# Window attention scores as stacked high and low halves, with the projections placed between the head pairs

## The chip, the cores and the metric

The kernel runs on one core of one Trainium2 chip. The metric is the device time of one execution in microseconds (us), the median of the runs shown. The engines are named as the profile names them: PE is TensorE (matrix products, PEld its weight loads), DVE is VectorE, ACT is ScalarE, POOL is GpSimd, SP is SyncE, which only issues DMA transfers here.

## The reference, cut to what matters

The program is two transformer blocks in a row on 256 latent and 256 context tokens, width 1024. The change lies in the mixer of the first block's first layer. There half of the width is attention with 8 heads of 64, the other half a Hyena operator (a short convolution, a gate, and a long convolution by Fourier transforms):

```python
qa_l, ka_l, va_l = [split_heads(t, NA_HEADS) for t in jnp.split(p_lat[..., :3 * NA_WIDTH], 3, axis=-1)]
qa_c, ka_c, va_c = [split_heads(t, NA_HEADS) for t in jnp.split(p_ctx[..., :3 * NA_WIDTH], 3, axis=-1)]
k_c = qk_norm(ka_c, k_gain)
a_lat = merge_heads(neighbourhood_attention(qk_norm(qa_l, q_gain), qk_norm(ka_l, k_gain), va_l,
                                            k_c, va_c, rpb))
b_lat = hyena_operator(p_lat[..., 3 * NA_WIDTH:], conv_w, conv_b, filter_params, d_bias)
o_lat = jnp.concatenate([a_lat, b_lat], axis=-1) @ w_out
...
a_ctx = merge_heads(dense_attention(qk_norm(qa_c, q_gain), k_c, va_c))
b_ctx = hyena_operator(p_ctx[..., 3 * NA_WIDTH:], conv_w, conv_b, filter_params, d_bias)
o_ctx = jnp.concatenate([a_ctx, b_ctx], axis=-1) @ w_out
```

Each latent query attends, in one softmax, to the latent tokens of its window (with a bias by relative position, minus infinity outside the window) and to all 256 context keys; each context query attends to the context keys. Queries and keys are normalised per head and multiplied by a gain. In the Hyena half, a projection gives x0, x1 and v; z = conv(v) * conv(x1) goes through the long convolution, and the result is multiplied by conv(x0).

## The kernel before, in words

All large matrix products run on pairs of float32r tiles, a high part and a low part of each operand (`split`), in three products each (`mm3`, L248 to L250). In what follows "a projection product" is one of these. Weights come by DMA from SP into `st` tiles (6 of them), and ACT (L210) and DVE (L211) split each into two `w` tiles; there are 11 `w` tiles. A block of 128 output features is 24 products of 512 columns and needs two `w` tiles.

`even_mixer` runs in this order of the program: v, q and k by token blocks of 128 (`proj_tok`); `qk_evac` takes the squares on ACT, the sums on DVE, the power on POOL and normalises on DVE; `turn` transposes a normalised block on PE into ring `pd` and DVE multiplies it by the gain, 128x128 at a time (L768), into `qT` and `kT`, which hold two heads above each other, 64 partitions each. Then x1's first two feature blocks (`project(4, x1_evac, 0)`), whose `conv` is a scaled copy on ACT (L782) and four updates on DVE (L785, L787).

Then come four pairs of heads. `lat_pair(j)` does the 256 latent queries in two halves of 128: for each of the two heads a score product of 64 rows and 512 columns in plain float32 (L253, from `mm4`) into ring `pb`; DVE adds the bias and takes the maximum (L828), takes the maximum of the context part (L832), combines and negates both (L833); ACT takes two exponentials with sums (L835, L836); DVE adds the sums, inverts and scales (L837 to L839); PE transposes (L842) into `pd`, ACT copies (L844), and when both halves are there PE multiplies by the values into ring `pc`. `ctx_pair(j)` does the same for context queries with scores of 256 columns. Every PSUM ring has two buffers, so the next two scores start when exponential and maxima of the last two have been read.

Behind the four pairs stand in the program `project(8, v2_evac, 0)`, `project(4, x1_evac, 1)`, `project(8, v2_evac, 1)` (48 projection products each), then the forward transform of z for the latent half (`forward(0)`: transposes, spectrum products, some 17 elementwise operations on DVE), the two blocks of x0, `inverse(0)`, `forward(1)`, `inverse(1)`, and the projection out (`project_out`).

The order in which each engine gets its instructions is set by a scheduler when the program is built: it takes, engine by engine, the first instruction in program order that it expects to be ready. On the chip every engine then works through its list in that order and waits where an operand is not there.

Of the kernel before, what the change touches and what calls it, by code (L numbers as in the profile page):

```python
# [11 lines left out]
FT = mybir.dt.float32  # L12
FR = mybir.dt.float32r
AF = mybir.ActivationFunctionType
# [102 lines left out]
T5 = 8  # L117
# [25 lines left out]
class Kernel:  # L143
# [593 lines left out]
    def even_mixer(self, hs):  # L737
        nc, d = self.nc, self.d
        w, wt = d["wf_even_in"], d["wt_even_in"]
        qT = [self.g() for _ in range(4)]  # L740
        kT = [self.g() for _ in range(4)]
        vt = [self.g() for _ in range(4)]

        pend = []

        def qk_evac(dst, gi):
            def f(u, p):
                if len(pend) == 3:
                    pend.pop(0)()
# [7 lines left out]
                n = self.t("5", bufs=T5)  # L757
                nc.vector.tensor_tensor(n.rearrange("p (h e) -> p h e", h=8), p.rearrange("p (h e) -> p h e", h=8),
                                        rs[:, :, None].to_broadcast([128, 8, 64]), op=OP.mult)
                pend.append(lambda: turn(dst, gi, u, n))  # L760
            return f

        def turn(dst, gi, u, n):
            pt = self.ps("d")
            for j in range(4):
                nc.tensor.transpose(pt[:, 128 * j:128 * j + 128], n[:, 128 * j:128 * j + 128], self.ident)
            for j in range(4):
                nc.vector.tensor_scalar(dst[j][:, 128 * u:128 * u + 128], pt[:, 128 * j:128 * j + 128],  # L768
                                        self.qkg[:, gi:gi + 1], None, op0=OP.mult)
# [5 lines left out]
        self.proj_tok(hs, wt[0], range(4), qk_evac(qT, 0), tags="ab")  # L775
        self.proj_tok(hs, wt[1], range(4), qk_evac(kT, 1), tags="ab")
# [32 lines left out]
        while pend:  # L809
            pend.pop(0)()  # L810

        cat = {}
        heads = [(hh, slice(64 * hh, 64 * hh + 64)) for hh in range(2)]

        def lat_pair(j):
            po = self.ps("c")
            PTs = [[self.t("5", bufs=T5).rearrange("p (a n) -> p a n", a=2) for _ in range(2)] for _ in range(2)]
            for qt in range(2):
# [3 lines left out]
                for hh, hp in heads:  # L822
                    self.mm4(ps[hh], qT[j][hp, 128 * qt:128 * qt + 128], kT[j][hp, :])
# [29 lines left out]
        def ctx_pair(j, po):  # L853
            PTs = []
            ps = [self.ps("b").rearrange("p (a n) -> p a n", a=2) for _ in range(2)]
            for qt in range(2):
                for hh, hp in heads:
                    self.mm4(ps[hh][:, qt, :], qT[j][hp, 256 + 128 * qt:384 + 128 * qt], kT[j][hp, 256:])
# [24 lines left out]

        for j in range(4):
            po = lat_pair(j)
            ctx_pair(j, po)
            cat[j] = self.pair(self.g, 512)
            self.split(po, *cat[j])

        project(8, v2_evac, 0)  # L890
        project(4, x1_evac, 1)
        project(8, v2_evac, 1)
# [588 lines left out]
```

## Time and profile before

| | before |
| --- | --- |
| median of 3 runs | 2512.43 us (2512.10 to 2514.53) |
| the profiled execution | 2512.93 us, span 2511.2 us |
| PE busy | 2478.3 us, 99% of the span |
| DVE busy | 1629.8 us, 65% |
| ACT busy | 1023.1 us, 41% |
| granted clock of PE, mean | 0.998 |
| q, k normalised to x1's first block done | 445.4 to 491.3 us |
| attention, then the three projections, to the spectrum | 491.3 to 585.0 us |
| transforms and x0, to the projection out | 585.0 to 631.8 us |

The page gives busy time per engine, the span in 40 slices, and groups of instructions; views of the trace give single instructions in order of time, busy time by stretch, and groups by shape. PE's products are pipelined: the time from one start to the next, not the duration in the row, is what a product costs on PE.

### The profile page before, as it was taken

The numbers are of one execution on the slowest core, as the hardware profiler recorded it, in microseconds if no ns is written. First come the engines' busy times: TensorE is split into PE (matmuls) and PEld (weight loads), VectorE is DVE, ScalarE is ACT, GpSimd is POOL, SyncE is SP. The second block draws the span as 40 slices with busy tenths as digits, with TensorE's granted clock in tenths as the row PEclk, the third lists the DMA queues.
The fourth block names the chain that finished last, engine by engine and source line by source line (L and its number), as shares of the span: only waits on it lengthen the run. The fifth ranks groups of instructions, "written<-read, shape, count | busy, mean of one in ns | idle before, by whom it ended". The sixth has DMA issues, their size and how long they took to land. (4 is left out here: it accounts for less than half of the span.)

```text
span 2511.2 us, 37305 instructions
## 1 busy us (share of the span) xinstructions
PE 2478.3 (99%) x14736; PEld 2166.0 (86%) x14736; DVE 1629.8 (65%) x2786; ACT 1023.1 (41%) x1599; POOL 55.3 (2%) x59
## 2 busy tenths in 40 slices
PE   8999999999999999999999999999999999999998
PEld 5887888757988888988888888889999999789998
DVE  5868666677876665855543656676557667776665
ACT  4322224363432222422222544455445446655544
POOL 0000000200000000000000000000000000100000
PEclk9999999999999999999999999999999999999999
DMA  8756543321365545464542333436656556544663
GB/s 308 230 154 191 161 151 115 92 71 52 112 190 165 166 150 157 132 207 152 175 131 80 118 101 112 141 129 194 185 168 194 185 170 204 171 136 135 202 184 92
DMA packets 117091, 386.97 MB, mean 154 GB/s; under 512 B 13603, under 2 KB 18868, under 8 KB 116916
## 3 DMA queue, kind: packets, MB, share of 16 engines
q1 hardware_dynamic: 116340, 383.53, 49.0%
q8 instruction: 116, 1.90, 0.3%
q10 hardware_dynamic: 576, 1.05, 0.1%
q14 instruction: 59, 0.48, 0.1%
HBM read 380.33 MB, written 2.10 MB: 152 GB/s over the span
## 5 line engine op out<-in xcount | busy, mean ns | idle before, releaser
L211 DVE TENSOR_TENSOR w<-st,w 128x1024 fp32r<-128x1024 f32 (+1 forms) x568 | 681.1, 1201 | 420.5 <-issue 158.7
L210 ACT ACTIVATE w<-st 128x1024 fp32r<-128x1024 f32 (+1 forms) x568 | 588.6, 1039 | 705.4 <-PE pc L250 331.9
L248 PE MATMUL pa<-h,w 128*128 128x256 f32 (+1 forms) x1560 | 515.3, 331 | 3.1 <-ACT h L369 2.4
L250 PE MATMUL pa<-h,w 128*128 128x256 f32 (+1 forms) x1560 | 514.3, 330 | 0.0
L248 PE MATMUL pc<-g,w 128*128 128x256 f32 (+1 forms) x1404 | 442.9, 316 | 2.7 <-DVE x L532 1.2
L249 PE MATMUL pa<-h,w 128*128 128x256 f32 (+1 forms) x1368 | 442.6, 324 | 0.3 <-DVE h L211 0.3
L249 PE MATMUL pc<-g,w 128*128 128x256 f32 (+1 forms) x1404 | 441.6, 315 | 0.0
L250 PE MATMUL pc<-g,w 128*128 128x256 f32 (+1 forms) x1404 | 441.2, 315 | 0.0
L300 DVE CUSTOM_DVE_ANT_0 junk<-st,cb,vec 128x1024 bf16<-128x1024 f32 x224 | 287.2, 1282 | 172.2 <-DMA st<-in_l_mod_dram 170.3
L248 PE MATMUL pb<-h,w 128*128 128x256 f32 (+1 forms) x1104 | 366.1, 332 | 0.0
L250 PE MATMUL pb<-h,w 128*128 128x256 f32 (+1 forms) x1104 | 365.7, 331 | 0.0
L248 PEld LDWEIGHTS pa<-h,w 128*128 128x128 f32 x1560 | 296.5, 190 | 34.3 <-ACT h L369 4.6
L250 PEld LDWEIGHTS pa<-h,w 128*128 128x128 f32 x1560 | 296.6, 190 | 30.7 <-issue 5.2
L249 PE MATMUL pb<-h,w 128*128 128x256 f32 (+1 forms) x912 | 294.4, 323 | 0.0
L248 PEld LDWEIGHTS pc<-g,w 128*128 128x128 f32 x1404 | 267.0, 190 | 22.0 <-DVE x L532 1.8
L249 PEld LDWEIGHTS pc<-g,w 128*128 128x128 f32 x1404 | 267.4, 191 | 16.8
L250 PEld LDWEIGHTS pc<-g,w 128*128 128x128 f32 x1404 | 267.2, 191 | 16.5
L249 PEld LDWEIGHTS pa<-h,w 128*128 128x128 f32 x1368 | 260.6, 191 | 23.7 <-issue 4.1
L250 PEld LDWEIGHTS pb<-h,w 128*128 128x128 f32 x1104 | 210.1, 190 | 20.4 <-issue 0.8
L248 PEld LDWEIGHTS pb<-h,w 128*128 128x128 f32 x1104 | 209.9, 190 | 19.9 <-issue 0.6
L249 PEld LDWEIGHTS pb<-h,w 128*128 128x128 f32 x912 | 173.9, 191 | 13.5 <-issue 0.2
L609 ACT ACTIVATE t<-pa 128x512 f32<-128x512 f32 (+1 forms) x92 | 48.7, 529 | 200.3 <-PE pa L250 200.2
(301 smaller groups left out, 2672.5 us busy)
## 6 DMA issues: line engine op xcount, KB each, us to landing
st<-in_l_mod_dram SPq DMA_DIRECT2D x128, 512.0 KB, 4.1
st<-in_wf_ffn_b_in_dram SPq DMA_DIRECT2D x88, 512.0 KB, 3.7
st<-in_wf_w_ffn_gu_dram SPq DMA_DIRECT2D x88, 512.0 KB, 3.7
st<-in_wf_ffn_a_in_dram SPq DMA_DIRECT2D x84, 512.0 KB, 4.4
st<-in_wf_ffn_a_out_dram SPq DMA_DIRECT2D x32, 512.0 KB, 3.8
st<-in_wf_ffn_b_out_dram SPq DMA_DIRECT2D x32, 512.0 KB, 3.6
st<-in_wt_ret_in_dram SPq DMA_DIRECT2D x32, 512.0 KB, 4.2
st<-in_wf_w_ffn_down_dram SPq DMA_DIRECT2D x32, 512.0 KB, 3.5
```

What stands on the lines that cost most here:

```text
L210: self.nc.scalar.activation(hi, src, AF.Copy)
L211: self.nc.vector.tensor_sub(lo, src, hi.bitcast(FT))
L248: mm(out, ll, rh, start=start, stop=False, skip_group_check=True)
L249: mm(out, lh, rl, start=False, stop=False, skip_group_check=True)
L250: return mm(out, lh, rh, start=False, stop=stop, skip_group_check=True)
L300: nc.vector.tensor_tensor_reduce(out=self.mp.tile([128, 1024], mybir.dt.bfloat16, name="junk", tag="junk"), in0=st, in1=self.cb[s], scale=1.0,
L609: nc.scalar.activation(s[:, sl], pss[j][0][:, sl], AF.Silu)
```

## The change

The scores are computed from tiles of 128 partitions. For each head, `stack(j)` writes the high part of q times gain into the head's own 64 partitions of a float32r tile (ACT, L772) and the low part into the other 64 (DVE, L773); the same for k into the `w` tile `keys`. A second `w` tile, `swap`, gets the keys with the two halves exchanged, by four DMA transfers of 64x512 (128 KB) per pair that ACT issues (L777, L778). A score is then two float32r products, q's stack with `keys` and with `swap` (`scores`), instead of one float32 product. The normalised q and k stay in `qn` and `kn` as they come (eight `g` tiles, as `qT` and `kT` were), and the transposes are done in `stack`, by pair. `stack(0)` and `stack(1)` stand ahead of the pairs, `stack(2)` and `stack(3)` behind the first and the second pair. The three projections that stood behind the pairs stand behind pair 0, 1 and 2. The heading under which the change goes also speaks of tiles of their own for the position biases; both versions load each bias into a tile of ring `t3`, and no line of the diff is about them.

The diff, with its context cut:

```diff
@@ -737,16 +737,12 @@
     def even_mixer(self, hs):
         nc, d = self.nc, self.d
         w, wt = d["wf_even_in"], d["wt_even_in"]
-        qT = [self.g() for _ in range(4)]
-        kT = [self.g() for _ in range(4)]
+        qn = [self.g() for _ in range(4)]
+        kn = [self.g() for _ in range(4)]
         vt = [self.g() for _ in range(4)]
 
-        pend = []
-
-        def qk_evac(dst, gi):
+        def qk_evac(dst):
             def f(u, p):
-                if len(pend) == 3:
-                    pend.pop(0)()
                 q = self.t("1")
                 nc.scalar.activation(q, p, AF.Square)
                 ss = self.small(8, "q")
@@ -754,26 +750,40 @@
                 nc.vector.tensor_scalar(ss, ss, 1.0 / 64, EPS, op0=OP.mult, op1=OP.add)
                 rs = self.small(8, "q")
                 nc.gpsimd.tensor_tensor(rs, ss, self.mhalf[:, :8], op=OP.pow)
-                n = self.t("5", bufs=T5)
-                nc.vector.tensor_tensor(n.rearrange("p (h e) -> p h e", h=8), p.rearrange("p (h e) -> p h e", h=8),
+                nc.vector.tensor_tensor(dst[u].rearrange("p (h e) -> p h e", h=8),
+                                        p.rearrange("p (h e) -> p h e", h=8),
                                         rs[:, :, None].to_broadcast([128, 8, 64]), op=OP.mult)
-                pend.append(lambda: turn(dst, gi, u, n))
             return f
 
-        def turn(dst, gi, u, n):
-            pt = self.ps("d")
-            for j in range(4):
-                nc.tensor.transpose(pt[:, 128 * j:128 * j + 128], n[:, 128 * j:128 * j + 128], self.ident)
-            for j in range(4):
-                nc.vector.tensor_scalar(dst[j][:, 128 * u:128 * u + 128], pt[:, 128 * j:128 * j + 128],
-                                        self.qkg[:, gi:gi + 1], None, op0=OP.mult)
+        heads = [(hh, slice(64 * hh, 64 * hh + 64), slice(64 - 64 * hh, 128 - 64 * hh)) for hh in range(2)]
+
+        def stack(j):
+
+            keys, swap = self.w(), self.w()
+            dsts = [self.f(FR) for _ in range(2)], [keys[:, 512 * hh:512 * hh + 512] for hh in range(2)]
+            for gi, (n, dst) in enumerate(zip((qn, kn), dsts)):
+                pt = self.ps("d")
+                for u in range(4):
+                    nc.tensor.transpose(pt[:, 128 * u:128 * u + 128], n[u][:, 128 * j:128 * j + 128], self.ident)
+                for hh, hp, op in heads:
+                    gain = self.qkg[hp, gi:gi + 1]
+                    nc.scalar.activation(dst[hh][hp], pt[hp], AF.Copy, scale=gain)
+                    nc.vector.scalar_tensor_tensor(dst[hh][op], pt[hp], gain, dst[hh][hp].bitcast(FT), op0=OP.mult,
+                                                   op1=OP.subtract)
+                    if gi:
+                        cols = slice(512 * hh, 512 * hh + 512)
+                        nc.scalar.dma_start(swap[hp, cols].bitcast(FT), keys[op, cols].bitcast(FT))
+                        nc.scalar.dma_start(swap[op, cols].bitcast(FT), keys[hp, cols].bitcast(FT))
+            return dsts[0], keys, swap
 
         def v_evac(u, p):
             nc.scalar.activation(vt[u], p, AF.Copy)
 
         self.proj_tok(hs, wt[2], range(4), v_evac)
-        self.proj_tok(hs, wt[0], range(4), qk_evac(qT, 0), tags="ab")
-        self.proj_tok(hs, wt[1], range(4), qk_evac(kT, 1), tags="ab")
+        self.proj_tok(hs, wt[0], range(4), qk_evac(qn), tags="ab")
+        self.proj_tok(hs, wt[1], range(4), qk_evac(kn), tags="ab")
         x0, z = {}, {}
 
         def conv(ch, p):
@@ -806,21 +816,23 @@
             self.proj_feat(hs, w, b0 + 2 * jp, full, lambda j, p: evac(2 * jp + j, p))
 
         project(4, x1_evac, 0)
-        while pend:
-            pend.pop(0)()
 
         cat = {}
-        heads = [(hh, slice(64 * hh, 64 * hh + 64)) for hh in range(2)]
-
-        def lat_pair(j):
+
+        def scores(p, hh, q0, k0, stacks):
+            q, *ks = stacks
+            for n, k in enumerate(ks):
+                self.mm4(p, q[hh][:, q0:q0 + 128], k[:, 512 * hh + k0:512 * hh + 512], n == 0, n == 1)
+
+        def lat_pair(j, stacks):
             po = self.ps("c")
             PTs = [[self.t("5", bufs=T5).rearrange("p (a n) -> p a n", a=2) for _ in range(2)] for _ in range(2)]
             for qt in range(2):
                 bias = self.t("3")
                 nc.sync.dma_start(bias, d["l_win"][j, qt])
                 ps = [self.ps("b") for _ in range(2)]
-                for hh, hp in heads:
-                    self.mm4(ps[hh], qT[j][hp, 128 * qt:128 * qt + 128], kT[j][hp, :])
+                for hh in range(2):
+                    scores(ps[hh], hh, 128 * qt, 0, stacks)
                 for hh in range(2):
                     p = ps[hh]
                     s = self.t("4")
@@ -850,12 +862,12 @@
                              k == 0, k == 3)
             return po
 
-        def ctx_pair(j, po):
+        def ctx_pair(j, po, stacks):
             PTs = []
             ps = [self.ps("b").rearrange("p (a n) -> p a n", a=2) for _ in range(2)]
             for qt in range(2):
-                for hh, hp in heads:
-                    self.mm4(ps[hh][:, qt, :], qT[j][hp, 256 + 128 * qt:384 + 128 * qt], kT[j][hp, 256:])
+                for hh in range(2):
+                    scores(ps[hh][:, qt, :], hh, 256 + 128 * qt, 256, stacks)
             for p in ps:
                 mx = self.small(2, "a")
                 nc.vector.tensor_reduce(mx, p, axis=AX, op=OP.max, negate=True)
@@ -881,15 +893,16 @@
                     self.mm4(po[64 * hh:64 * hh + 64, 256:], vt[2 + k][:, 64 * h:64 * h + 64], PTs[hh][:, k, :],
                              k == 0, k == 1)
 
+        stacks = [stack(j) for j in range(2)]
         for j in range(4):
-            po = lat_pair(j)
-            ctx_pair(j, po)
+            po = lat_pair(j, stacks[j])
+            ctx_pair(j, po, stacks[j])
             cat[j] = self.pair(self.g, 512)
             self.split(po, *cat[j])
-
-        project(8, v2_evac, 0)
-        project(4, x1_evac, 1)
-        project(8, v2_evac, 1)
+            if j < 3:
+                project(*((8, v2_evac, 0), (4, x1_evac, 1), (8, v2_evac, 1))[j])
+            if j < 2:
+                stacks.append(stack(j + 2))
 
         CS, CSt = self.g(), self.g()
         nc.sync.dma_start(CS, d["t_dft"][0])
```

Three places in the order, as built.

PE at the end of x1's first projection, before: `pa` are projection products, `pb` scores, L766 the last transposes of k.

```order
L766 MATMUL pd<-cst,t_3885 128x128 x4
L250 MATMUL pa<-h,w 128x512
L248 MATMUL pa<-h,w 128x512
L249 MATMUL pa<-h,w 128x512
L250 MATMUL pa<-h,w 128x512
L248 MATMUL pa<-h,w 128x512
L253 MATMUL pb<-g 128x512 x2
L249 MATMUL pa<-h,w 128x512
```

The same place now, from the last product of that projection to the next one: L769 transposes for a stack, `pb<-w,f` are score passes, L854 transposes of probabilities, `pc` the first value product.

```order
L250 MATMUL pa<-h,w 128x512
L769 MATMUL pd<-cst,g 128x128 x8
L253 MATMUL pb<-w,f 128x512
L769 MATMUL pd<-cst,g 128x128 x8
L253 MATMUL pb<-w,f 128x512 x5
L854 MATMUL pd<-cst,t_3973 128x128 x4
L253 MATMUL pb<-w,f 128x512 x2
L253 MATMUL pb<-w,f 128x256 x4
L854 MATMUL pd<-cst,t_3991 128x128 x4
L854 MATMUL pd<-cst,t_4017 128x128 x4
L253 MATMUL pc<-t_3961,g 64x256
L248 MATMUL pa<-h,w 128x512
```

Nineteen projection products stood between x1's projection and the first score before (the piece shows the last five of them); now none stands among the 40 instructions from there to the first value product.

DVE at the beginning of the second pair, before: L861 to L869 end the first pair's context softmax, L828 is bias and maximum of the second pair's first scores.

```order
L861 TENSOR_REDUCE sa<-pb 128x2
L867 RECIPROCAL sa<-sa 128x2
L869 TENSOR_SCALAR t_4093<-t_4093,sa 128x256 x2
L867 RECIPROCAL sa<-sa 128x2
L869 TENSOR_SCALAR t_4109<-t_4109,sa 128x256 x2
L828 ISA t_4142,sa<-pb,t_4136 128x256
L828 ISA sa 128x1
L832 TENSOR_REDUCE sa<-pb 128x1
L833 TENSOR_SCALAR sa<-sa 128x1
```

DVE at the same place now: L795 and L797 are conv updates of the projection that has just ended, L810 its product with x1, L773 the low parts of a stack, L840 bias and maximum, L211 a weight split.

```order
L797 SCALAR_TENSOR_TENSOR t_4180<-pa,vec,t_4180 128x255
L795 SCALAR_TENSOR_TENSOR t_4180<-pa,vec,t_4180 128x255
L773 SCALAR_TENSOR_TENSOR f<-pd,qkg,f 64x512
L797 SCALAR_TENSOR_TENSOR t_4180<-pa,vec,t_4180 128x255
L773 SCALAR_TENSOR_TENSOR w<-pd,qkg,w 64x512
L810 TENSOR_TENSOR f<-t_4180,f 128x512
L773 SCALAR_TENSOR_TENSOR f<-pd,qkg,f 64x512
L840 ISA t_4226,sa<-pb,t_4218 128x256
L840 ISA sa 128x1
L773 SCALAR_TENSOR_TENSOR w<-pd,qkg,w 64x512
L844 TENSOR_REDUCE sa<-pb 128x1
L211 TENSOR_TENSOR w<-st,w 128x1024
```

The pair's first softmax step followed the last one of the pair before; now ten instructions of the projection and of the stack stand ahead of it and a weight split behind it.

PE at the beginning of the third pair now (ahead of it stand the 24 products of a projection block):

```order
L769 MATMUL pd<-cst,g 128x128 x8
L253 MATMUL pb<-w,f 128x512 x4
L248 MATMUL pa<-h,w 128x512
L249 MATMUL pa<-h,w 128x512
L253 MATMUL pb<-w,f 128x512 x2
L854 MATMUL pd<-cst,t_4477 128x128 x4
```

Between the first and the second pair of scores stand two or three projection products; the others of the same block ended just ahead.

## Rows read from the trace of the kernel before

**Rows 1.** The page, busy time of each engine over the whole span.

```profile
PE 2478.3 (99%) x14736; PEld 2166.0 (86%) x14736; DVE 1629.8 (65%) x2786; ACT 1023.1 (41%) x1599; POOL 55.3 (2%) x59
```

**Rows 2.** Busy time by stretch; the first line names the columns.

```profile
core 0: us, PE busy (x) PEld busy (x) DVE busy (x) ACT busy (x) POOL busy (x), PEclk, DMA share, GB/s
491.28:585.00 93.72, 93.34 (x438) 58.32 (x436) 65.06 (x199) 54.20 (x157) 0.00 (x0) 1.00 0.24 74
585.00:631.80 46.80, 45.28 (x216) 35.08 (x216) 41.81 (x81) 14.83 (x24) 2.58 (x2) 1.00 0.15 46
632.00:652.00 20.00, 20.00 (x168) 19.92 (x168) 12.97 (x24) 5.02 (x10) 0.00 (x0) 1.00 0.39 110
50.00:60.00 10.00, 7.64 (x27) 6.08 (x27) 8.85 (x17) 6.41 (x10) 0.00 (x0) 0.83 0.49 152
```

**Rows 3.** Timeline of PE in the attention: start, duration, operation, shape, count.

```profile
489.24 0.39 PE L248 MATMUL pa<-h,w 128*128 128x512 f32 x1
489.46 0.39 PE L249 MATMUL pa<-h,w 128*128 128x512 f32 x1
...
491.28 1.03 PE L766 MATMUL pd<-cst,t 128*128 128x128 f32 x8
492.07 0.47 PE L248 MATMUL pa<-h,w 128*128 128x512 f32 x1
...
497.06 1.13 PE L253 MATMUL pb<-g 64*128 64x512 f32 x4
498.12 0.50 PE L249 MATMUL pa<-h,w 128*128 128x512 f32 x1
...
506.10 1.13 PE L253 MATMUL pb<-g 64*128 64x256 f32 x4
507.15 0.50 PE L250 MATMUL pa<-h,w 128*128 128x512 f32 x1
...
509.77 0.65 PE L253 MATMUL pc<-t,g 128*64 128x256 f32 x2
...
511.22 1.12 PE L253 MATMUL pb<-g 64*128 64x512 f32 x2
512.27 1.94 PE L253 MATMUL pc<-t,g 128*64 128x256 f32 x14
```

**Rows 4.** Groups by line and shape: second block's stacks (2115 to 2200), gains (443 to 500).

```profile
L1197 DVE TENSOR_TENSOR g<-t,g 64x512 fp32r<-64x512 f32 x16 | 11.0, 687 | 3.0 <-ACT g L1196 2.7
L1196 ACT ACTIVATE g<-t 64x512 fp32r<-64x512 f32 x16 | 10.0, 628 | 4.3 <-DVE t L1191 4.1
...
L768 DVE TENSOR_SCALAR g<-pd,qkg 128x128 f32<-128x128 f32 x32 | 9.1, 343 | 2.3 <-PE pd L766 2.2
```

**Rows 5.** DMA: KB and us to landing; issue time on ACT's queue in ns.

```profile
g<-g SPq DMA_DIRECT2D x32, 64.0 KB, 3.0
...
L685 ACTq DMA_DIRECT2D spec<-t x2: 326/336/345, 257.5 to 262.9; - x2
```

**Rows 6.** Groups by line and shape, 491.28 to 585: busy us, mean ns.

```profile
L211 DVE TENSOR_TENSOR w<-st,w 128x1024 fp32r<-128x1024 f32 x7 | 8.6, 1223 | 9.4 <-PE pa L248 9.4
...
L835 ACT ACTIVATE t<-pb,sa 128x256 f32<-128x256 f32 x16 | 7.6, 476 | 3.7 <-DVE sa L833 3.2 <-DVE sa L837 0.4
...
L828 DVE CUSTOM_DVE_ANT_0 t<-pb,t 128x256 f32<-128x256 f32 x16 | 6.8, 423 | 9.1 <-PE pd L873 3.9 <-PE pd L842 3.0 <-PE pb L253 2.0
L832 DVE TENSOR_REDUCE sa<-pb 128x1 f32<-128x256 f32 x16 | 6.7, 418 | 0.0
...
L787 DVE SCALAR_TENSOR_TENSOR t<-pa,vec,t 128x255 f32<-128x255 f32 x8 | 3.8, 480 | 0.2
...
L782 ACT ACTIVATE t<-pa,vec 128x512 f32<-128x512 f32 x4 | 3.1, 777 | 8.3 <-PE pa L250 8.3
```

**Rows 7.** Timeline of DVE behind the spectrum, from its first operation on.

```profile
587.98 0.69 DVE L698 SCALAR_TENSOR_TENSOR t<-t,pb 128x512 f32<-128x512 f32 x1 [4.21 <-PE pb L253]
588.59 0.68 DVE L918 TENSOR_TENSOR t<-pb,g 128x512 f32<-128x512 f32 x1
```

## The prediction

> **What bounds the kernel now.** I read the page's busy line first, then the windows of the mixer, then PE's instructions there in order of time. PE is busy 99% of the span, DVE 65%, ACT 41% [rows 1]; the reader is to see that PE work which is removed is time won only where PE stays busy. The windows say it of the stage that the change touches: from 491.28, where x1's first projection ends, to 585.0, where the spectrum of z begins, PE is busy 93.34 of 93.72 us; from there to 631.8, where the projection out takes over, 45.28 of 46.80, with DVE busy 41.81 of that [rows 2]. So PE bounds the attention, because projections lie ready to fill it, and behind the attention DVE is close under PE. The chain of waits has no line over 1% and points to no place.
>
> **PE work.** Before, a head's score over 64 contraction rows is one float32 product, two records each. The first four records start at 497.06 and the next product at 498.12: both heads of the pair in 1.06 us. A head alone takes as long, 511.22 to 512.27 [rows 3]. Of the eight such pairs (four pairs of heads, two query halves) only the first runs together in the timeline, the other fourteen heads one by one: 1.06 + 14 x 1.05 = 15.8 us. The 16 context scores of 256 columns take 1.05 for two (506.10 to 507.15): 8.4. Together 24.2.
>
> After, each head has two float32r passes over 128 rows. Such a product of 512 columns starts 0.22 to 0.23 us behind the last (489.24, 489.46) [rows 3]; one of 256 every 20.00 / 168 = 0.119 [rows 2]. 32 x 0.228 + 32 x 0.119 = 11.1. The transposes stay 32, by pair instead of by token block, at 0.1 each (eight from 491.28 to 492.07). PE thus loses **13.1 us** of work.
>
> The two heads that ran together at 497.06 show what stacking gives up, since one 128-row product fills the array alone [rows 3]. The Trainium skill, TensorE: Matmul & The Clock Gate, section Part 3 (Packing small matmuls), recommends the reverse of this change, products with few contraction rows on separate row groups so that they run at once. Were all 32 scores of before paired so, before would hold 8 x 1.06 + 8 x 0.53 = 12.7 us of them and the forecast below would stand 11.5 higher; the trace shows one pair of eight running together and decides for 13.1.
>
> **ACT and DVE work.** The stacks add 16 high parts on ACT (64x512, 0.628 each) and 16 low parts on DVE (0.687), by the same operations in the second block; DVE gives back 32 gains of 0.343 [rows 4]: 11.0 against 11.0, nothing. ACT gains 10.0 and 16 DMA issues, which on its queue take some 0.33 [rows 5]: 15.3 us beside its 54.20 of 93.72 [rows 2]. None of it is on the path while PE has other work. What matters is where it stands, and when PE has none.
>
> **Hole 1, the first pair.** PE's order shows it: behind x1's last product stand 16 transposes, twelve score passes and twelve transposes, and no projection until the first value product; before, 19 projections stood ahead of the first score and eleven behind it. The missing fill, project(8, ...), is now later in the program than the whole pair, and it needs four of the eleven w tiles while the stacks of two pairs hold four.
> From T, the end of x1's projection, ACT's copy takes 0.78, three conv updates on DVE 1.44, q's low part 0.69, another update 0.48, k's low part 0.69 [rows 4, 6]; with 0.1 for the drain of the last product T + 4.2, before the first pass can start. The swapped copy of the keys is then issued on ACT, 0.33, and lands some 3.0 later, as the second block's half as large copies do [rows 5]: T + 7.5 for the second pass. From finished scores to the first value product the old pair needed 498.12 to 509.77, 11.65 [rows 3], with the same softmax steps and the same table load in it. So T + 19.2. PE's work in that time is 28 transposes 2.8, eight passes 1.8, four of 256 columns 0.5: 5.1. Hole: **14 us**. Bounds: 10, if the old 11.65 is partly waiting behind fill; 18, if the second pair's stack (4 x 0.628 and four issues on ACT, 4 x 0.687 on DVE), which stands amid this chain, lies wholly on it.
>
> **Holes 2 and 3, pairs two and three.** The projections between the pairs do not help a pair's beginning, since they stand ahead of its scores and end just there. PE then has eight transposes, four passes and three projections, 2.4 us, until a score buffer of ring pb is free again. Ahead of that stand, in DVE's row, four conv updates (0.48 each), four low parts (0.69), a product with x1 (0.68), bias and maximum (0.42 and 0.42) and a weight split (1.22) before the maximum is negated; ACT's copy of 0.78 goes ahead, an exponential of 0.48 follows [rows 4, 6, 7]. Sum 8.7, less about 0.08 for each of ten starts, as DVE's instructions overlap (587.98 and 588.59 for one of 0.69) [rows 7]: 7.9. Hole **5.5**; the third pair has no such product, **4.9**. Bounds 3 and 9 each: the split may come earlier, or ACT's DMA issue that waits for DVE's last low part holds up what stands behind it. The fourth pair has no stack in front and its fill is complete: 0, at most 3.
>
> **Hole 4, the transforms.** The fill that the pairs now use up is missing behind the spectrum: by PE's order 127 products of 512 columns stood there, 76 do now, 51 x 0.228 = 11.6 us less. PE alone would end that stretch in 46.8 - 11.6 = 35.2. But DVE's chain does not shrink: 41.81 us busy, less three weight splits that have moved ahead (five to two, 3.7), and it begins 3.0 behind the spectrum (587.98) [rows 2, 6, 7]: 41.1. So **5.9 us** of it are late. Bounds 0, if more of it overlaps, and 9.
>
> **Sum.** 14 + 5.5 + 4.9 + 5.9 - 13.1 = +17.2. The profiled execution took 2512.93 (span 2511.2); 2530.1, and the median of before is 0.5 below the profiled one: **2530 us**, slower by 0.7%. With all bounds low 10 + 6 + 0 - 13.1 = +2.9, 2515; with all high 18 + 18 + 3 + 9 - 13.1 = +34.9, 2547.
>
> **Rivals.**
> *The holes do not open*: 2512.4 - 13.1 = **2499**. ACT and DVE would have to finish the stacks within the last projection, and the softmax chain be half its 11.65. For it: before, PE idles only 0.38 us in the whole attention [rows 2]. Against: that was due to fill, and PE takes its instructions in the order in which they stand. It decides from 13.1: PE's idle time from T to the projection out below that means faster. Chance 0.12.
> *Holes near their lower ends*, about 13 in all: **2512**, no difference. For it: the walk adds durations, and engines overlap. 0.15.
> *The clock falls in the holes*: in 50 to 60, where PE was busy 7.64 of 10.00, the granted clock was 0.83, so 1.2 GHz for a third of it [rows 2]. In the first pair 5 us of PE work would take up to 10, half of it on the chain, and at each later hole 1 to 3: +6 to +12, **2539**. By the Trainium skill, TensorE: Matmul & The Clock Gate, section Why this matters for your kernels, gaps between bursts bring the half clock back; the row agrees. 0.2.
> *The change does not do what it says*: no line of the diff touches the bias tiles; that part costs 0 and changes no case.
>
> **How the numbers follow.** Forecast 0.48, the clock 0.2, no difference 0.15, faster 0.12, beyond 2546 by late swapped copies 0.05. A measurement of this kernel can tell about 0.2%, 5 us. Slower 0.73, same 0.15, faster 0.12. The range 2509 to 2546 leaves out the faster case, the last one and a rim of the middle one.
>
> **What would show it.** Right: PE waits for DVE, ACT or a DMA for some 14 us between x1's last product and the next projection, the first 3 us of it on the low part of the keys; two waits of about 5 us at the fronts of pairs two and three, ended by an exponential behind a weight split; PE some 34 us busy of 41 between the spectrum and the projection out; score passes of 0.23 us. Wrong: no PE wait over 2 us there, or passes of 0.45 and more, which would take the saving away without any hole. A granted clock below 1.00 there speaks for the third rival.

## The result, and the profile after

The changed kernel takes 2539.66 us (median of 4 runs, 2539.18 to 2541.34) against 2512.28 for the kernel before (4 runs): 1.0111 times, 95% interval 1.0099 to 1.0123. Measured again beside the later experiments it was 1.0115 (1.0100 to 1.0130). The forecast was 2530 with a range of 2509 to 2546; slower was forecast, and the range holds the time.

The page, busy time of each engine, to set beside [rows 1]. Nothing is to be seen there: PE does the same share of work.

```profile
PE 2479.6 (98%) x14736; PEld 2175.3 (86%) x14736; DVE 1633.9 (64%) x2770; ACT 1033.8 (41%) x1615; POOL 54.1 (2%) x59
```

The windows show where it happens. Cut at the first value product, the spectrum, the projection out and the beginnings of pairs two, three and four (columns as in [rows 2]: length; busy time and instructions of PE, PEld, DVE, ACT, POOL; granted clock of PE; DMA share; GB/s):

```profile
488.10:508.86 20.76, 10.68 (x41) 7.21 (x40) 14.51 (x37) 13.24 (x29) 0.00 (x0) 0.71 0.25 64
508.86:528.00 19.14, 19.10 (x88) 13.98 (x89) 8.35 (x20) 7.05 (x20) 0.00 (x0) 0.87 0.24 69
528.00:559.70 31.70, 24.64 (x122) 17.74 (x121) 19.29 (x52) 16.41 (x43) 0.00 (x0) 0.89 0.25 67
559.70:590.00 30.30, 24.00 (x120) 17.28 (x119) 22.44 (x55) 19.75 (x47) 0.00 (x0) 0.89 0.40 122
590.00:617.40 27.40, 27.38 (x143) 20.64 (x142) 19.45 (x54) 17.22 (x44) 0.00 (x0) 1.00 0.42 135
617.40:659.80 42.40, 36.34 (x165) 28.31 (x165) 37.19 (x72) 11.69 (x21) 2.99 (x2) 0.88 0.09 26
```

The same piece of work before, from x1's last projection product to the projection out, in one row:

```profile
491.05:631.80 140.75, 138.86 (x654) 93.54 (x653) 107.07 (x280) 69.03 (x180) 2.58 (x2) 1.00 0.21 65
```

In four stretches of six PE idles, and in five the granted clock is below 1.00. PE's four longest waits between 440 and 664 of the changed kernel, longest total first (engine, tile, line; what it waited for; us, times, longest):

```profile
PE pa L248 <- DVE w L211: 13.4, 2, 7.0
PE pc L253 <- DVE t L941: 5.1, 1, 5.1
PE pb L253 <- DVE w L773: 3.5, 1, 3.5
PE pd L854 <- DVE t L851: 2.4, 1, 2.4
```

The sum, by PE. The piece takes 171.7 now and took 140.75, 31.0 more; it begins 3.0 earlier (488.1 against 491.05), mostly because 20 transposes of q and k that stood ahead of that point, 2.0 us of PE's work, moved behind it; so the projection out begins 28.0 later, at 659.81 against 631.82. The rest of the program is the same within 0.4: spans 2539.6 and 2511.2. PE's idle time is 171.7 - (10.68 + 19.10 + 24.64 + 24.00 + 27.38 + 36.34) = 29.6 now and 1.9 before: **+27.7**. PE's busy time is 142.1 now and 138.9 before, +3.3. In that are the score passes, -13.1 by the forecast, and the moved transposes, +2.0; what is left is 3.3 + 13.1 - 2.0 = **+14.4**. Nearly all of it is the same work at the lower clock. These are the stretches of the piece in which the granted clock is 0.50, the second one cut at the first value product:

```profile
493.47:496.88 3.41, 3.03 (x10) 1.96 (x10) 2.10 (x5) 1.75 (x4) 0.00 (x0) 0.50 0.45 103
500.29:508.86 8.57, 4.88 (x18) 3.79 (x19) 5.46 (x18) 5.84 (x18) 0.00 (x0) 0.50 0.32 87
508.86:513.95 5.09, 5.09 (x14) 3.66 (x15) 3.61 (x9) 3.02 (x10) 0.00 (x0) 0.50 0.74 198
534.43:541.25 6.82, 4.22 (x12) 3.35 (x13) 5.29 (x15) 3.54 (x10) 0.00 (x0) 0.50 0.67 172
565.15:571.97 6.82, 4.03 (x11) 3.08 (x12) 6.55 (x20) 5.50 (x14) 0.00 (x0) 0.50 0.63 173
643.65:653.89 10.24, 6.59 (x29) 6.30 (x30) 9.73 (x17) 0.75 (x2) 0.00 (x0) 0.50 0.29 89
```

PE is busy 27.8 us in them, which is some 13.9 more than the same work would take at 1.00. Of these, 4.0 lie ahead of the first value product, where PE still waits between its products, and 10.0 behind the waits, where one product follows another.

### The profile page after: what moved, and what is told of

Its sections match the earlier page's. It is cut to its first block, busy times and chain, and to the rows that moved or that the text cites. A ratio compares the mean times of both kernels' runs of the same rounds, so it can differ in the third digit from the quotient of the medians.

```text
span 2539.6 us, 37350 instructions
## 1 busy us (share of the span) xinstructions
PE 2479.6 (98%) x14736; PEld 2175.3 (86%) x14736; DVE 1633.9 (64%) x2770; ACT 1033.8 (41%) x1615; POOL 54.1 (2%) x59
## 5 line engine op out<-in xcount | busy, mean ns | idle before, releaser
L211 DVE TENSOR_TENSOR w<-st,w 128x1024 fp32r<-128x1024 f32 (+1 forms) x568 | 681.3, 1202 | 411.4 <-issue 158.1
L248 PE MATMUL pa<-h,w 128*128 128x256 f32 (+1 forms) x1560 | 516.7, 332 | 16.4 <-DVE w L211 14.1
L250 PEld LDWEIGHTS pc<-g,w 128*128 128x128 f32 x1404 | 267.2, 191 | 16.4
```

What stands on the lines that cost most here:

```text
L211: self.nc.vector.tensor_sub(lo, src, hi.bitcast(FT))
L248: mm(out, ll, rh, start=start, stop=False, skip_group_check=True)
L250: return mm(out, lh, rh, start=False, stop=stop, skip_group_check=True)
```

## The experiments

Three theories stood against each other. **A**: the stacks' tiles stand ahead of the projections' weights in ring `w`; the scheduler's order takes tiles of a ring in program order, so the weights are split late and PE has nothing to fill its waits with. **B**: the place of the projections between the pairs is at fault. **C**: the stacks' own work on DVE, ACT and the copies lies on the path wherever the projections stand. Every ratio is to the kernel before measured beside that run on the same chip: 2512.28 for the changed kernel, 2510.7 to 2511.2 for the others. One table of all runs; the events are starts on PE in each profiled execution, and the idle time is PE's from 440 to the projection out.

| run | time, us | ratio (95%) | first value product | spectrum | projection out | PE idle |
| --- | --- | --- | --- | --- | --- | --- |
| before | 2512.28 | 1 | 509.8 | 585.0 | 631.8 | 1.9 |
| changed | 2539.66 | 1.0111 (1.0099 to 1.0123) | 508.9 | 617.4 | 659.8 | 29.6 |
| e0 changed again | 2539.59 | 1.0115 (1.0100 to 1.0130) | 507.9 | 617.2 | 659.7 | 29.2 |
| e1 stacks, old order | 2536.02 | 1.0099 (1.0084 to 1.0114) | 508.7 | 606.8 | 653.6 | 22.5 |
| e2 projections only | 2518.72 | 1.0031 (1.0018 to 1.0044) | 507.0 | 592.6 | 636.0 | 5.7 |
| e3 swap on SP | 2535.86 | 1.0098 (1.0083 to 1.0113) | 511.8 | 610.9 | 653.3 | 26.8 |
| e6 weights first | 2513.25 | 1.0008 (0.9998 to 1.0017) | 508.6 | 590.0 | 630.2 | 11.3 |
| e9 transform early | 2515.84 | 1.0020 (1.0011 to 1.0030) | 509.2 | 571.9 | 635.1 | 11.8 |
| e11 before, transform early | 2524.09 | 1.0052 (1.0035 to 1.0069) | 507.7 | 569.7 | 642.7 | 7.0 |
| e12 useless filler | 2540.04 | 1.0118 (1.0103 to 1.0133) | 508.8 | 612.7 | 655.1 | 21.4 |
| e13 weights first, filler | 2514.77 | 1.0012 (1.0004 to 1.0021) | 512.1 | 590.6 | 633.5 | 12.3 |
| e14 filler, transform early | 2515.27 | 1.0016 (1.0007 to 1.0025) | 509.4 | 570.3 | 631.7 | 13.3 |
| e15 filler, low parts on POOL | 2519.80 | 1.0033 (1.0020 to 1.0046) | 511.7 | 598.9 | 641.5 | 17.7 |
| e17 filler, first stack early | 2512.95 | 1.0007 (0.9998 to 1.0016) | 510.2 | 588.3 | 631.7 | 11.7 |

**e1: the projections back behind the four pairs.**

```diff
-            if j < 3:
-                project(*((8, v2_evac, 0), (4, x1_evac, 1), (8, v2_evac, 1))[j])
             if j < 2:
                 stacks.append(stack(j + 2))
+        project(8, v2_evac, 0)
+        project(4, x1_evac, 1)
+        project(8, v2_evac, 1)
```

> The changed kernel with the three projections put back behind the four pairs, all else kept. Theory A, the ring of w tiles decides: its tiles are handed out in program order, and a weight that stands behind the tiles of a stack gets none before that stack has taken its own. Then the projections stand behind stacks 2 and 3 and cannot fill the first pairs: PE idles some 10 in the first pair's beginning as in the changed kernel, some 4 more in its end, 5 to 8 in each of pairs two and three (work of 10.1 per pair in a chain of up to 18), while the wait of 5.1 behind the spectrum goes: 2512.4 - 13.1 + 26 + 3 for the clock = 2528, 2518 to 2545. Theory B, the place of the projections between the pairs decides: behind the pairs they are free filler as in the kernel before, all holes close, 2499 to 2505. Theory C, the stacks' own work (low parts, swapped copies) lies on the path wherever the projections stand: about 2535 with the same waits at pairs two and three.

Measured 2536.02. Behind the pairs, where they were filler in the kernel before, the projections fill nothing: the first product of one starts at 551.4, after two pairs have gone by. The windows of this run:

```profile
488.00:510.00 22.00, 12.28 (x44) 7.71 (x43) 14.88 (x39) 13.56 (x33) 0.00 (x0) 0.63 0.28 72
510.00:545.00 35.00, 26.33 (x125) 17.13 (x126) 21.30 (x66) 20.35 (x60) 0.00 (x0) 0.74 0.15 42
606.80:653.50 46.70, 45.18 (x216) 35.05 (x216) 41.78 (x81) 14.81 (x24) 2.59 (x2) 1.00 0.15 46
```

PE idles 9.7 in the first stretch and 8.7 in the second, and its clock falls to 0.63 and 0.74. The stretch behind the spectrum is the one of before again, 46.70 against 46.80 in [rows 2], with no hole. B falls (it asked for 2499 to 2505). C had the time, 2535, but not the picture: the two waits of 7 and 6 at pairs two and three are gone. A has the picture, and its range holds the time, 8 above its middle. What was too small in that middle is the clock, put at 3: in this run PE is busy 30.1 us in stretches whose granted clock is 0.50, half of which, 15, is what the lower clock adds to its work.

**e2: the kernel before with the projections alone moved.**

```diff
             self.split(po, *cat[j])
+            if j < 3:
+                project(*((8, v2_evac, 0), (4, x1_evac, 1), (8, v2_evac, 1))[j])
-        project(8, v2_evac, 0)
-        project(4, x1_evac, 1)
-        project(8, v2_evac, 1)
```

> The kernel before with only the three projections moved behind pairs 0, 1 and 2; scores stay plain float32, no stacks, no swapped copies. Theory A (ring order): no stack holds or precedes w tiles, so weights are split ahead and the projections fill the pairs: PE full, 2512 within 4. Theory B (place in the program): holes of some 8 in the first pair, 4 each at pairs two and three, 6 behind the spectrum, and 5 for the clock without any saving: 2535. Theory C (stacks' own work): 2512.

Measured 2518.72, 0.31% slower. None of the three numbers was right. No wait is left in the pairs (the longest there is 0.3), so the place of the projections opens no hole by itself and B falls again; but the hole behind the spectrum is there without any stack:

```profile
PE pc L253 <- DVE t L926: 4.2, 1, 4.2
PE pc L253 <- DVE t L929: 1.0, 1, 1.0
```

In the kernel before the same two waits were 0.2 and 1.0. So most of this hole belongs to the order of the projections: here too they are used up in the pairs (from the spectrum to the projection out 101 products of 512 columns are left, 143 before), and the spectrum begins at 592.6 instead of 585.0.

**e6: the weights' tiles taken ahead of the next stack's.** `proj_feat` and `project` are given weights that are already loaded and split:

```diff
+        early = [self.wblocks(w, 8)]
         stacks = [stack(j) for j in range(2)]
...
-                project(*((8, v2_evac, 0), (4, x1_evac, 1), (8, v2_evac, 1))[j])
+                project(*((8, v2_evac, 0), (4, x1_evac, 1), (8, v2_evac, 1))[j], early[j])
             if j < 2:
+                early.append(self.wblocks(w, (6, 10)[j]))
                 stacks.append(stack(j + 2))
```

> The changed kernel with one thing moved: the w tiles of each projection are taken and split ahead of the next stack's in the program (project(8,..,0) ahead of stack(0), the next two ahead of stack(2) and stack(3)); products, stacks, passes and pairs keep their places. Theory A: projections fill the first pair and the fronts of pairs two and three, the granted clock stays 1.00 there, and only the wait behind the spectrum is left, some 6: 2512.4 - 13.1 + 6 = 2505, 2500 to 2511. Theory B: the projections keep their place in the program, so holes of 10, 7 and 6 stay: 2535 or more. Theory C: the first softmax of pairs two and three still stands behind conv updates and low parts on DVE, waits of about 7 and 6 stay and the first pair's 10 partly: 2520 to 2535.

Measured 2513.25: 26 of the 27 us are gone with the products, stacks, passes and pairs at their places. The holes at pairs two and three are closed, and of the first pair's 10.1 there are 2.8 left. That is A's mechanism, late weights, and it excludes C for these holes, since C kept the waits of 7 and 6. The weight splits of DVE (L211) agree: between 474 and 508 the changed kernel has none (e1 none up to 530), while the kernel before and e2 have seven between 473 and 500, and e6 has two more than the changed kernel, at 473.6 and 477.0. (Whether the means is the ring or only the place of the weights in the program is not shown: e6 moves their loading and splitting forward together with their tiles, no row of a trace names a ring, and no run had more `w` tiles.) A's number was missed, 2505 (2500 to 2511): the windows of this run,

```profile
500.00:520.00 20.00, 16.79 (x88) 11.29 (x87) 15.96 (x45) 14.46 (x40) 0.00 (x0) 0.91 0.28 84
520.00:540.00 20.00, 19.98 (x109) 14.98 (x108) 16.93 (x51) 14.17 (x43) 0.00 (x0) 1.00 0.37 106
590.00:630.00 40.00, 32.06 (x150) 24.63 (x150) 34.93 (x67) 10.33 (x20) 2.59 (x2) 0.87 0.07 25
```

and the two products behind the spectrum that wait,

```profile
617.86 1.19 PE L253 MATMUL pc<-g,t 128*128 128x128 f32 x4 [7.42 <-DVE t L943]
619.57 5.31 PE L253 MATMUL pc<-g,t 128*128 128x128 f32 x28 [0.52 <-DVE t L946]
```

show it. PE's idle time up to the projection out is 11.3, 9.4 more than before. Busy time from x1's end to the projection out is (630.2 - 487.2) - 11.3 = 131.7, 7.2 less than before's 138.9; -13.1 for the scores and +2.0 for the transposes leave +3.9, which fits the lower clock: PE is busy 8.5 at 0.50 here, half of it 4.3. The saving of 13.1 is there, and 9.4 + 3.9 are spent on idle time and clock. (The projection out starts 1.6 earlier than in the kernel before, but the program behind it takes 1.9 longer, 1881.3 for 1879.3; why was not looked for.)

**e3: the swapped copies issued by SP.** In `stack`, `nc.scalar.dma_start(swap...)` becomes `nc.sync.dma_start(swap...)`.

> The changed kernel with the 16 swapped copies issued by SP instead of ACT. Theory A: ACT loses 5.3 of issues, of which little is on the path; PE's wait for a copy was 0.9: 2537 to 2540. Theory C in the form that the issues on ACT, which wait for DVE's last low part, hold up the exponentials: holes two and three shrink by some 2 each and the first by 2, 2533 or less.

Measured 2535.86, ratio 1.0098 against 1.0115 and 1.0111 of the changed kernel; the intervals overlap. PE's wait for a copy falls from 0.9 to 0.2, and that for the weights' low parts stays (13.4, twice, in the changed kernel; 16.4, three times, here). Who issues the copies is worth 4 at most; between A's 2537 and C's 2533 it does not decide.

**e0 and e12: the changed kernel again, and the same with useless work in the first hole.**

```diff
             ctx_pair(j, po, stacks[j])
+            if j == 0:
+                idle = self.ps("a")
+                for _ in range(44):
+                    self.mm4(idle, hs[0][0][:, :128], hs[0][0])
```

> The changed kernel itself, beside the others on one chip. 1.0111 times before was measured; the same within 0.2% is expected, 2535 to 2541, with PE's waits of 7, 6 and 5 at pairs two and three and behind the spectrum, and the granted clock near 0.51 between 500 and 512.

> The changed kernel with 44 products of 512 columns added (10.0 at 0.228) that nothing reads, as filler behind the first pair; they stand in PE's row between the stack's transposes, the score passes and the first transposes of probabilities, where PE idled. If the half clock costs time by itself: the chain from T to the first value product stays at 20.5 or gets a little shorter, the granted clock there goes from 0.5 to near 1.00, the products behind it start 0.23 apart instead of 0.43, and the time falls 3 to 6 below the changed kernel's, although PE has 10 more work. If only the idle time counts: unchanged within 2. If the filler stands in the way: up to 10 more.

Measured 2539.59 and 2540.04, no difference in the total. Within the mixer there is one. From 493.4 to 499.4, first the changed kernel (e0), then with the filler (e12), whose last useless product stands at the end of this stretch:

```profile
493.40:499.40 6.00, 3.78 (x9) 2.03 (x9) 4.46 (x12) 3.99 (x7) 0.00 (x0) 0.50 0.24 56
```

```profile
493.40:499.40 6.00, 6.00 (x31) 5.00 (x29) 4.95 (x12) 4.02 (x7) 0.00 (x0) 1.00 0.49 128
```

The granted clock is 1.00 instead of 0.50, that is 2.4 instead of 1.2 GHz, and it stays so up to 529. But the filler does more than was expected: the scheduler's order changes with it, and 13 real projection products now stand ahead of the first value product, where the changed kernel has none. So between 500 and 512, where the granted clock is 1.00 against 0.50 too, PE is kept busy by real products and not by useless ones. The first value product does not come earlier (508.8 and 507.9); since filler and projections stand ahead of it, that does not tell what the lower clock costs in the chain of the first pair. The projection out starts 4.6 earlier, but 3.5 of that are lost again behind it in the profiled execution: PE idles 2.0 more there, and the granted clock is 0.95 instead of 1.00 in the first 35 us. The medians do not confirm a gain. So that PE kept busy by useless work keeps the higher clock is shown; that it saves time in the whole is not.

**e9 and e11: the forward transform ahead of the fourth pair**, in weights first, and in the kernel before (with the projections moved as in e2): the tables and `ys = forward(0)` stand at the top of the loop for j = 3.

> Weights first, as before, and in addition the forward transform of the latent half (with its tables) ahead of the fourth pair in the program instead of behind it. Theory A: the wait of 7.4 behind the spectrum comes from DVE's chain that has no filler left beside it; beside the fourth pair and x0's products it is hidden, the clock stays 1.00: 10 below weights first, 8 below before, 2500 to 2506. Rival: DVE bounds attention and transforms together (82 of 102 and 35 of 40 busy in weights first), the chain only moves: within 3 of weights first, about 2511.

> The kernel before (plain scores, no stacks) with both moves of program order: projections behind pairs 0, 1, 2 and the forward transform ahead of the fourth pair. If what the moves repair is only a hole that the change opened, PE is full as in before: 2511 within 4, so the saving of the transform-early run is the score passes' own. If the early transform is a gain of its own: 2506 or less.

Measured 2515.84 and 2524.09. For e9 only the rival's number fits, for e11 neither. Theory A fails here in the form that only missing filler makes the last hole: the chain moves, as its rival said. Two waits of e9, at the fourth pair's scores and behind the spectrum, show where to:

```profile
587.09 0.73 PE L253 MATMUL pb<-w,f 128*128 128x512 f32 x2 [3.30 <-ACT t L847]
621.81 0.68 PE L253 MATMUL pc<-g,t 128*128 128x128 f32 x4 [3.25 <-DVE t L925]
```

One wait of 7.4 has become two of 3.3. In the kernel before, the same move costs 5 more than e2, 0.52% in all; it is no gain of its own, and where these 5 go was not looked for.

**e13, e14, e15, e17: four attempts at the rest.** In e13 the projections get a lower priority, so that the scheduler treats them as standing behind the four pairs, with the weights ahead as in e6:

```diff
             if j < 3:
-                project(..., early[j])
+                with self.tc.high_priority((-760, -520, -280)[j]):
+                    project(..., early[j])
```

e14 adds e9's move to it. e15 lets POOL do the low parts of the weights of these projections (`nc.gpsimd.tensor_tensor` instead of `nc.vector.tensor_sub`); those of x0, which the expectation counts too, stay on DVE, since the edit switches back ahead of them: six low parts, not ten. e17 takes the weights of x1's first projection and of the next one first and puts `stack(0)` ahead of x1's projection.

> Weights first, and the three projections' instructions given a lower priority, so that the scheduler places them behind the four pairs as in the kernel before, while their weights keep their place ahead of the stacks. What is left of the change is then the stacked scores alone. Theory PE bounds: pairs are no longer held up by the projection ahead of them, attention ends earlier, the wait of 7.4 behind the spectrum shrinks to 2 or less, 13.1 - 3 below before: 2501, 2498 to 2506. Theory DVE's and ACT's chain of attention and transforms bounds (DVE 117 busy of 142 in weights first): the wait only moves, within 3 of weights first, 2510 to 2515.

> The filler run with the forward transform ahead of the fourth pair. Theory PE bounds: 2498 to 2506. Theory the chain bounds: the fourth pair's softmax stands behind the transform's 17 operations on DVE as in the transform-early run, a wait of about 3 there and 4 behind it, 2512 to 2517.

> The filler run with the low parts of the weights of the three projections and x0 (ten splits of 1.22 on DVE) done by POOL, which is idle here. If DVE's chain bounds: DVE loses up to 12 of work, 4 to 8 below the filler run. If not: within 2 of it, or slower where POOL's low parts come late (a 128x1024 operation on POOL takes an estimated 2.6, twice the 1.29 of its 128x512 one behind the spectrum).

> The filler run with the weights of x1's first projection taken first, then stack(0), then that projection, so that the first stack's chain of 7.5 runs beside x1's products. If the attention chain bounds from T on: up to 7 earlier, 4 to 7 below the filler run. If PE bounds: within 2 of it.

Measured 2514.77, 2515.27, 2519.80 and 2512.95. None is below the kernel before. e13 and e14 go as the theory of the chain said; e17 brings 1.8, not 4 to 7, which its expectation had given to PE as the bound. e15 does not fit the simplest form of that theory: between 440 and 664 the six low parts went to POOL,

```profile
L237 POOL TENSOR_TENSOR w<-st,w 128x1024 fp32r<-128x1024 f32 x6 | 14.2, 2381 | 41.4 <-PE pd L860 20.8 <-ACT w L236 20.6
```

2.38 us each against 1.22 on DVE, and the kernel became 5 slower than e13, not faster: PE idles 17.7. The trace shows a cost of the move itself. A small operation of the softmax on DVE, 0.16 us elsewhere, lasts 1.58 and ends at 508.96, just as POOL's two low parts do:

```profile
504.27 4.67 POOL L237 TENSOR_TENSOR w<-st,w 128x1024 fp32r<-128x1024 f32 x2 [20.83 <-PE pd L860]
507.38 1.58 DVE L855 TENSOR_TENSOR sa<-sa 128x1 f32<-128x1 f32 x1 [1.18 <-ACT t L854]
```

Beside POOL's other low parts the same happens twice: 1.31 for that operation, up to 534.28 (POOL up to 534.26), and 2.27 for a small one of the normalisation (L756), 0.16 elsewhere. Other operations of DVE beside POOL's keep their length. Together the three are some 4.7 us longer than usual. Whether it makes up the 5 is not shown, and e15 so does not settle whether the amount of DVE's work holds these versions.

What stays open: no version tried beats the kernel before; e6 and e17 equal it. In e6, e13 and e17 PE idles 11 to 12 before the projection out, 5 to 8 of it in one wait for DVE behind the spectrum. Which dependency would have to be shortened so that the 13.1 come through was not found.

## Why the prediction was right, and where its size was off

**PE's work, -13.1: right, as far as it can be read.** The four passes of pair four, at full clock, take 591.22 - 590.31 = 0.91, 0.228 each as worked out; four of 256 columns take 0.54 to 0.72 at full clock, a little more than the 0.48 worked out:

```profile
590.31 1.07 PE L253 MATMUL pb<-w,f 128*128 128x512 f32 x4
591.22 0.39 PE L248 MATMUL pa<-h,w 128*128 128x512 f32 x1
```

**Hole 1: the walk was right, its division into idle time and work was not.** T is 488.3, where ACT's copy starts. Timeline of PE from x1's last product to the first products of a projection (in brackets, idle time before and what ended it):

```profile
488.09 1.04 PE L769 MATMUL pd<-cst,g 128*128 128x128 f32 x8
492.62 0.50 PE L253 MATMUL pb<-w,f 128*128 128x512 f32 x1 [3.49 <-DVE w L773]
493.50 1.09 PE L769 MATMUL pd<-cst,g 128*128 128x128 f32 x4 [0.38 <-DVE f L773]
494.74 1.08 PE L769 MATMUL pd<-cst,g 128*128 128x128 f32 x4 [0.15 <-DVE w L773]
495.47 1.20 PE L253 MATMUL pb<-w,f 128*128 128x512 f32 x2
497.57 0.51 PE L253 MATMUL pb<-w,f 128*128 128x512 f32 x1 [0.90 <-DMA w<-w]
499.44 0.74 PE L253 MATMUL pb<-w,f 128*128 128x512 f32 x2 [1.36 <-ACT t L847]
502.60 1.09 PE L854 MATMUL pd<-cst,t 128*128 128x128 f32 x4 [2.42 <-DVE t L851]
...
508.86 1.11 PE L253 MATMUL pc<-t,g 128*64 128x256 f32 x2 [0.47 <-ACT t L856]
509.90 0.80 PE L248 MATMUL pa<-h,w 128*128 128x512 f32 x1
510.50 0.63 PE L249 MATMUL pa<-h,w 128*128 128x512 f32 x1
510.92 0.63 PE L250 MATMUL pa<-h,w 128*128 128x512 f32 x1
...
514.40 0.40 PE L248 MATMUL pa<-h,w 128*128 128x512 f32 x1
514.64 0.39 PE L249 MATMUL pa<-h,w 128*128 128x512 f32 x1
```

The reader sees the first pass at T + 4.3 (T + 4.2 forecast) after a wait for DVE's low part, the first second pass at T + 7.2 (T + 7.5), the first value product at T + 20.6 (T + 19.2). From the second pass to the first value product it took 13.4, not the 11.65 of the kernel before; the second pair's stack and the lower clock both stand in it, and no run separates them. Idle are 10.1, the lower bound, not 14, because PE's own work in that time took not 5.1 but 10.7 (the first window of the changed kernel). 4.0 of the 5.6 between them are the lower clock; the rest is that products which stand alone last longer, as the first pass with 0.50 instead of 0.228.

The forecast gave two reasons for the missing filler. That the projections stand later in the program than the pair is not enough: e2 has the same place and full pairs. The second, that the stacks hold the tiles which the weights need, is what the experiments bear out, with the open question named at e6: e6 keeps place and stacks, takes the weights first, and leaves 2.8 of the hole.

**Holes 2 and 3: right, a little short.** 7.05 and 6.30 for 5.5 and 4.9, within the bounds. PE and DVE at the second pair:

```profile
528.81 1.17 PE L253 MATMUL pb<-w,f 128*128 128x512 f32 x4
537.03 0.79 PE L248 MATMUL pa<-h,w 128*128 128x512 f32 x1 [7.05 <-DVE w L211]
```

```profile
534.04 0.42 DVE L840 CUSTOM_DVE_ANT_0 t<-pb,t 128x256 f32<-128x256 f32 x1
...
535.29 0.42 DVE L844 TENSOR_REDUCE sa<-pb 128x1 f32<-128x256 f32 x1
535.75 1.23 DVE L211 TENSOR_TENSOR w<-st,w 128x1024 fp32r<-128x1024 f32 x1
536.89 0.21 DVE L845 TENSOR_SCALAR sa<-sa 128x1 f32<-128x1 f32 x1
```

The row of DVE came as forecast, with the split ahead of L845. What ends the wait is the split itself, since the projection product that stands next on PE needs that weight; the forecast had counted three such products as available and named the exponential. Those three products, 0.7, were not there, and the walk from ACT's copy (528.22) to the exponential's end (537.66) took 9.4 instead of 7.9; against that the wait ends 0.7 ahead of the exponential's end.

**Hole 4: right, in part by chance.** 5.13 + 0.52 + 0.41 = 6.1 for 5.9. The stretch was 1.3 longer than forecast (42.4 for 41.1) and PE busy 1.1 longer (36.3 for 35.2, 3.3 of it the lower clock), and the two cancel. Of the five weight splits of before, three still lie in it and a fourth begins at its end, where the forecast left two; DVE is busy 37.2 all the same, 38.1 forecast. e2 shows that the order of the projections alone makes most of the hole, 5.2.

**The clock: the term that the sum lacked.** It was a rival at 0.2 with +6 to +12, 2539, and not part of the forecast. PE's work took some 13.9 longer by it. Products that start 0.23 apart at 514.40 start 0.43 apart at 510.50, so work behind a hole pays too: 2.5 behind the first, 2.1 and 2.0 behind the next two, 3.3 behind the last, which is near the "1 to 3" of the rival for the later holes. The rival had nothing behind the first hole. Inside it, it counted 2.5; half of the busy time there at the lower clock is 4.0, but slow products and waits share one stretch there, of 20.6 from T where 19.2 were forecast, so no more than 1.4 of these can stand on top of the forecast. The Trainium skill, TensorE: Matmul & The Clock Gate, section Why this matters for your kernels, says that gaps between bursts of products bring the half clock back; all four holes of this trace agree.

**The sum.** The holes' idle time was forecast as 30.3 and is 29.6. That this is so near is chance: the first is 3.9 shorter, partly because slow work fills it, and the next two together are 3.0 longer. 1.9 of idle time were there before and were not taken off. From the forecast's +17.2 to the +28.0 of the projection out lead the clock, +13.9, the idle time, 27.7 - 30.3 = -2.6, the earlier start with its moved transposes, 2.0 - 3.0 = -1.0, and 0.5 that is not assigned. So the middle of the forecast, 2530, is 9.7 short mainly because the clock was put at nothing there; the range holds the time because it was wide enough for the rival, on whose number, 2539, the time fell.

**The rivals.** "The holes do not open" asked for less than 13.1 of idle time; e6 got there (11.3) and still did not reach 2499, since what idle time is left and the lower clock take up the 13.1. "Near their lower ends", 2512, is where e6, e13 and e17 are. Late swapped copies did not come: they land in 2.2, one wait of 0.9. The part on the position biases did nothing, as said.

## What to carry to other kernels

Work that PE no longer has to do is worth time only as long as PE has other work at each of its waits; here 13 us of PE time were saved, and every version that closed the holes only came back to the time of before. When a change takes tiles from a ring that also feeds the filler, look at the order in which the ring's tiles are taken: with two tiles per stack ahead of the weights the kernel took some 26 us more than with the weights taken and split first. Price each hole together with the slow products behind it.

## What the runs showed of the hardware

In and behind four holes of 6 to 10 us of idle time PE was busy 27.8 us at the granted clock of 0.50, where its products start 0.43 apart instead of 0.23; that is some 13.9 us more of PE's time, about half as much as the holes themselves. Useless products in the first hole kept the granted clock at 1.00 from 493.4 to 499.4, where it was 0.50, but brought no measurable gain in the total. POOL takes 2.38 us for an elementwise operation of 128x1024 that takes DVE 1.22, and three times a small operation on DVE, 0.16 us elsewhere, lasted 1.31 to 2.27 and ended when POOL's operation did.
